# Hybrid DeltaNet / gMLP block: squares of W1 tied behind the level copies of the inverse, rows of the second MLP half loaded later

## The chip, the cores and the metric

The kernel runs on one core of a Trainium2 chip. The core has five engines that run side by side, each with its own list of instructions in a fixed order: TensorE (PE, matrix products), VectorE (DVE), ScalarE (ACT), GpSimd (POOL) and SyncE (SP, which here issues the loads and stores). The metric is the device time of one execution in microseconds; lower is better. The time before is the median of three executions.

## The reference, cut to what matters

One layer runs over 128 context tokens and 2048 latent tokens (17 tiles of 128), all in float32. What bears on the change:

```
h   = rmsnorm(x) * (1 + scale1) + shift1
qkv, gate, ab, u, vg = split(h @ w_in)
o_a = gated DeltaNet, forward and backward over chunks of 64   # triangular solve per chunk, then a scan
o_b = gelu(u) * (w_spatial @ layernorm(gelu(vg)) + b_spatial)
x   = x + gate1 * (concat(norm(o_a) * silu(gate), o_b) @ w_out)
h   = rmsnorm(x) * (1 + scale2) + shift2
x   = x + gate2 * (square(relu(h @ w_ff1)) @ w_ff2)
y   = rmsnorm(x) * norm_final
```

The outputs are the new context rows, the new latent rows and the final states of the context scan.

## The kernel before, in words

**Stages.** (1) The input stage: six blocks of up to three tiles are normalised, projected to q, k and v, convolved, and put into DRAM (`qT_d`, `kT_d`, `kt_d`, `vt_d`, and the products `kk_d`, `qk_d`). Its last steps (`decay_steps`) turn the decay inputs into cumulative sums `gcol`, transpose them on PE (L779) and store them as rows in `g_d` (L784). (2) The scan stage: a first pass over 17 units (forward direction) and a second over 17 (backward). Each unit inverts a 128 x 128 triangular matrix per head, in `prep`, by doubling levels of 2, 4, 8, 16, 32 and 64, and then takes four `scan` steps. A unit's inverse begins with the load `gb` of its decay rows from `g_d` (L1104); ACT makes `E` of it (L1166, L1167), POOL masks it, DVE multiplies it into `KK`, and a copy and a transpose later PE starts level 2 (L1218). Each level is: PE, a DVE product with a mask (L1222), PE (L1231, L1233), and two ACT copies, `Y` (L1234) and `X` (L1235); the last of these is the level copy that the change speaks of. (3) The first MLP product, in two halves of token tiles with seven products each (steps in the order 1, 5, 6, 7, 3, 2, 4 for each unit of 256 columns, class `Unit`), reading the row tiles `hop`. Step 5's sum is copied out of its bank of PSUM by ACT (L1768), and step 3 adds onto that same bank, so that step 3 waits for the copy. (4) The second MLP product.

Each product of full precision is three matmuls on split operands (`mm3`, L313 to L315).

**Fill.** While the inverses run, PE is given other products to do: in the first pass the projections to gate, u and vg from `hrow` rows (the "fill"), of which 111 matmuls stand ahead of the first inverse; in the second pass the output projection with W_out.

**Squares of W1.** The MLP's first product needs a power of two for scaling w_ff1, and with it the sum of squares over that whole matrix. So 64 pieces of 256 KB are loaded into `raw` buffers (`w1_load`, four buffers in turn, shared with W_out's pieces), and ACT squares each and sums it (`square_w1`, L247). `w1_range` takes the sum and makes the scale. Only this scale is needed, and not before the MLP.

**What sets the order.** The scan stage's steps are given times in units of a scan step (`at`), and are recorded in that order. A scheduler then orders each engine's list by its own model of time: an instruction may move ahead of one recorded earlier if its inputs are ready, unless a tie forbids it. Two helpers write ties between instructions of one engine: `behind` (behind all instructions kept under a name) and `calm` (behind the last level copy recorded on that engine). They add no wait on the chip, only an order. Before the change, loads and squares of W1 have times of 0.5 and 1.0 onward, and no tie.

**The second half's MLP rows.** The context tile's rows `h2_d[0]` are stored by `h2_steps` (L1006) and read back by `first_load` (L1808, two loads of 256 KB, each split into two 16-bit parts by ACT at L1680 and DVE at L1673). It is called 20 steps ahead of the second half (`half - 20`). The second half's `hop` tiles are loaded by `hop_next` (L1071) from step `half - 11` on.

Of the kernel before, what the change touches and what calls it, by code (L numbers as in the profile page):

```python
# [62 lines left out]
def hybrid_step(  # L63
# [121 lines left out]
    def raw_w(src, pool=None, tag="w"):  # L185
        t = (pool or wp).tile([P, 512], F32, tag=tag, name="raw")
        load(out=t, in_=src)
        return t
# [24 lines left out]
    done = {}  # L213
# [32 lines left out]
    def square_w1(n, raw):  # L246
        A.activation(raw, raw, AF.Square, accum_out=w1_sums[:, n : n + 1])  # L247
# [26 lines left out]
    def here():  # L274
        return len(tc.nc.cur_bb.bb.instructions)

    def behind(name, start, engines):

        for x in tc.nc.cur_bb.bb.instructions[start:]:
            for y in done[name]:  # L280
                if x.engine == y.engine and x.engine in engines:
                    tc.add_manual_dep(x, y.name, mybir.DependencyInfo(
                        mybir.DependencyClass.NoSync, mybir.DependencyReason.DATA), reason="order")
# [13 lines left out]
    def w512(name, dt=F32):  # L297
        return wp.tile([P, 512], dt, tag="w", name=name)
# [77 lines left out]
    with ExitStack() as ph:  # L376
# [104 lines left out]
        for t in BLOCKS[0]:  # L481
            x = pe.tile([P, D], F32, tag="x", name="x", bufs=6)
# [410 lines left out]
        for bi in range(len(BLOCKS)):  # L893
# [4 lines left out]
            at = {e: n for n, e in enumerate(order)}  # L898
            tile_of = {}
            for n, (gi, h) in enumerate(order):  # L900
                u = us[n] if bi == 0 and n < 3 else feature_tile(blk, bi, gi, h)
# [157 lines left out]
    def hop_tile(dt, n):  # L1059

        side, bufs = ("A", 2) if n else ("B", 5)
        shape = [P, 2, 4, 2, 4, P] if dt == F16 else [P, 4, 2, 4, P]
        return hops[side].tile(shape, dt, tag="hop", name="hop", bufs=bufs)

    def hop_next():
        g, o = hop_order.pop(0)
        if g == 0:
            both = hop_tile(F16, o in ORDER[:2])
            hop[0, o], hop[1, o] = both[:, 0], both[:, 1]
        for k in range(0, 4, 2):  # L1070
            load(out=hop[g, o][:, k : k + 2], in_=hop_d[g, o][:, k : k + 2])  # L1071


    with ExitStack() as ph:
# [44 lines left out]
        def calm(f, lag=0):  # L1119

            start = here()
            f()
            for x in tc.nc.cur_bb.bb.instructions[start:]:
                if x.engine in urgent and len(urgent[x.engine]) > lag:
                    tc.add_manual_dep(x, urgent[x.engine][-1 - lag].name, mybir.DependencyInfo(
                        mybir.DependencyClass.NoSync, mybir.DependencyReason.DATA), reason="order")
# [309 lines left out]
        w1_raws = {}  # L1436

        def w1_load(n):
            k, fb = divmod(n, 8)
            w1_raws[n] = raw_w(w_ff1[0, k * P : (k + 1) * P, fb * 512 : fb * 512 + 512], sp, "raw")  # L1440
# [15 lines left out]
        def load_wo(n, k):  # L1456
            if k == 0:
                ga1.append(wrow(mod_d[1:2, 2 * D + n * 512 : 2 * D + n * 512 + 512]))
                WO.append([])
            WO[n].append(load_split(w_out[0, k * P : (k + 1) * P, n * 512 : (n + 1) * 512], wscale[:, k : k + 1]))  # L1460

        def o_loads(u):
            t = u["t"]
            u["of"], u["ga"] = w512("of"), w512("ga")
            load(out=u["of"], in_=of_d[t * P : (t + 1) * P, :])
            load(out=u["ga"], in_=gate_d[t * P : (t + 1) * P, :])
# [74 lines left out]
        def at(time, fn, kind=None):  # L1541
            events.append((time, len(events), fn, kind))

        def spread(t0, t1, steps, kind):
            for j, st in enumerate(steps):
                at(t0 + (t1 - t0) * (j + 0.5) / len(steps), st, kind)

        def scan_step(i, f):
            def g():
                u = units[i]  # L1550
                if "s" not in u:
                    u["s"] = None if i in (0, NT) else units[i - 1]["sn"] if i not in (1, NT + 1) else u["s0"]
                f()
            return g

        def after(i):

            d = 0 if i == 0 else 1
            store(out=new_state[0, 0, d].rearrange("h k v -> k h v"), in_=units[i]["sn"])

        def state_load(i):

            s0 = fpart("s0").rearrange("p (h d) -> p h d", h=H)
            load(out=s0, in_=state_delta[0, 0, 0 if i == 0 else 1].rearrange("h k v -> k h v"))
            units[i + 1]["s0"] = s0

        def noted(name, f):

            start = here()
            f()  # L1570
            done[name] = tc.nc.cur_bb.bb.instructions[start:]

        def after_keys(f):

            start = here()
            f()
            behind(("kk", 1), start, (mybir.EngineType.SP,))

        p2, p3 = WINDOWS[:8], WINDOWS[8:]
        for i, u in enumerate(units):  # L1580
            w = p2 if i <= NT else p3
            at(i - 3 if i > 1 else -12.1, lambda i=i, u=u: noted(("kk", i), u["prep_loads"]))
            at(i - 3 if i > 1 else -11.1, (lambda u=u: after_keys(u["qk_load"])) if i < 2 else u["qk_load"])
            at(i - 1, u["scan_loads"])
            n = len(u["prep"])
            for j, st in enumerate(u["prep"]):
                at(i - w[0] + (j + 0.5) * (w[0] - w[1]) / n if i or j > 9 else -11.6 if j < 2
                   else 0.2 * j - 8.15, st, "prep")
            for j, f in enumerate(u["scan"]):
                shift = {2: 0.12}.get(j, 0.0) if i > NT else 0.0  # L1590
                at(i + w[2] + (w[3] - w[2]) * (j + 0.5) / 4 + shift, scan_step(i, f), "chain")
            if i in (0, NT):
                at(i - 1, lambda i=i: state_load(i))
                at(i + w[2] + (w[3] - w[2]) * 0.7, lambda i=i: after(i))
            if i >= NT:
                at(i, lambda u=u: o_loads(u))
                first, second = o_steps(u)
                spread(i + p3[4], i + p3[5], first, "fill")
                spread(i + p3[6], i + p3[7], second, "fill")
                if u["t"] > 8:  # L1600
                    st = h2_steps(u["t"], pj, fraw, w512, fpart, fhalf, lambda u=u: u["x2"])
                    spread(i + p3[8], i + p3[9] + 0.2, st[:5], "fill")
                    spread(i + p3[9] + 0.2, i + p3[9] + 2.1, [lambda f=f: calm(f) for f in st[5:]], None)
# [19 lines left out]
        flat = flat[NF:]  # L1623
        spread(p2[4], p2[5], flat, "fill")
        for n in range(64):
            at(0.5 + n * 0.24, lambda n=n: w1_load(n))
            at(1.0 + n * 0.24, lambda n=n: square_w1(n, w1_raws.pop(n)))
        at(16.5, w1_range, "fill")
        wo = [lambda n=n, k=k: load_wo(n, k) for n in range(2) for k in range(KT)]
        spread(16.75, 17.4, wo[:6], None)  # L1630
        spread(17.45, 18.2, wo[6:], None)
# [66 lines left out]
    def as4(t):  # L1698
        return t.rearrange("p (a d) -> p a d", a=4)
# [105 lines left out]
    def first_load():  # L1805
        for i in range(2):
            r = as4(w512("x0"))
            load(out=r, in_=h2_d[0][:, i * 4 : i * 4 + 4, :])  # L1808
            h, lo = split16x4(r)
            x0.extend((h[:, k, :], lo[:, k, :]) for k in range(4))  # L1810
# [264 lines left out]
    def weights_at(p):  # L2075
        if p < len(seq):
            o, n, b = seq[p]
            units[n].weights(o)

    def loads_at(p):  # L2080
        if p < len(seq) and seq[p][1] not in begun:
            begun.add(seq[p][1])
            units[seq[p][1]].loads()
# [7 lines left out]
    half = [p for p, e in enumerate(seq) if e[1] == NP][0]  # L2091
    later = []
    for j, t in enumerate(range(8, -1, -1)):
        st = h2_steps(t, bank, lambda: w512("junk"), w512)
        p = 10 + 19 * j // 2
# [7 lines left out]
    for p, (o, n, b) in enumerate(seq):  # L2103
        u = units[n]
        loads_at(p + LEAD + 8)
        weights_at(p + LEAD)
        while later and later[0][0] <= p:
            later.pop(0)[1]()
        if p == half - 20:
            first_load()  # L2110
        u.step(o)
        while firsts and firsts[0][0] <= p:
            firsts.pop(0)[2]()
        if half - 11 <= p < half + 3 and (half - p) % 2:
            hop_next()
        e = p - last
        if e >= 0 and e % 2:
            if e // 2 == 0:
                for m in range(AHEAD):
                    s_next(m, True)  # L2120
                t_ahead(0, 4)
            elif e // 2 < 5:
                for k in range(4 * (e // 2) - 4, 4 * (e // 2)):
                    t_next(0, k)
                if e // 2 <= AHEAD:
                    s_next(e // 2 - 1, False)
                    s_next(AHEAD + e // 2 - 1, True) if e // 2 < 3 else None
# [107 lines left out]
```

## Time and profile before

| what | value |
|---|---|
| time, median of 3 | 2556.02 us (2554.91 to 2556.05) |
| the profiled execution's own time | 2553.04 us |
| its span in the trace | 2551.3 us |
| PE busy | 2468.6 us, 97% |
| DVE busy | 1888.3 us, 74% |
| ACT busy | 1342.8 us, 53% |
| POOL busy | 235.7 us, 9% |
| DMA share | 67.8% of 16 engines' span |

Busy time is the time in which an engine had an instruction under way. The granted clock of TensorE is 0.988 of full speed over the span. Times below are microseconds from the span's start. An idle time in brackets is the time that the engine sat idle just before the instruction, with what ended it.

### The profile page before, as it was taken

Reading aid. Unit: us, or ns where it says so; the run is one execution under the profiler, and the core shown is the slowest. Engines: PE = TensorE matmul, PEld = TensorE weight load, DVE = VectorE, ACT = ScalarE, POOL = GpSimd, SP = SyncE. Lnnn points to the kernel's source line nnn. Section 1 sums busy time; section 2 is a strip of 40 time slices with the busy share of each in tenths; the row PEclk is TensorE's granted clock in tenths of the full one; section 3 lists DMA queues with packets and bytes.
Section 4 is the critical chain, followed back from the end, with each engine's and each line's share of the span. In section 5 each row is a group of like instructions: output and inputs, shape, how many; then the busy total and the mean of one; then the engine's idle time right before and its main releaser. Section 6 shows DMA issues by size and latency. Waiting matters only on the chain.

```text
span 2551.3 us, 44102 instructions
## 1 busy us (share of the span) xinstructions
PE 2468.6 (97%) x15188; PEld 1664.4 (65%) x15188; DVE 1888.3 (74%) x3898; ACT 1342.8 (53%) x3257; POOL 235.7 (9%) x429
## 2 busy tenths in 40 slices
PE   8999998599999999999999989999999999999998
PEld 4666666266666688778544434444467888888887
DVE  4868885387777888987688968878775557785875
ACT  3756766565555667764365645555443433243442
POOL 3112211111111111110000000000000000000000
PEclk9999999799999999999999999999999999999999
DMA  8767757844444656675567786666589979786773
GB/s 290 229 181 216 226 161 229 277 155 152 143 138 132 187 175 229 225 250 181 188 203 237 235 250 191 196 179 187 159 273 371 337 265 320 254 263 206 226 258 112
DMA packets 480487, 554.04 MB, mean 217 GB/s; under 512 B 37812, under 2 KB 284892, under 8 KB 480262
## 3 DMA queue, kind: packets, MB, share of 16 engines
q1 hardware_dynamic: 480262, 551.22, 67.8%
q8 instruction: 119, 1.95, 0.3%
q14 instruction: 106, 0.87, 0.1%
HBM read 395.00 MB, written 156.08 MB: 216 GB/s over the span
## 4 chain that ended last, share of the span: by engine, by line
PE 79%; DMA 8%; DVE 6%; ACT 4%; issue 1%; SPq 1%; POOL 1%; POOLq 0%; DVEq 0%; ACTq 0%
PE f L313 16%; PE f L314 16%; PE f L315 16%; PE pj L313 5%; PE pj L315 5%; PE pj L314 5%; PE pd L1138 5%; DMA raw<-in_w_ff_dram 2%; PE pm L313 2%; PE pm L314 2%; PE pm L315 2%; DMA QK<-qk_d 1%; PE pt L683 1%; DMA raw<-in_w_mod_dram 1%; DMA t_d<-r 1%
## 5 line engine op out<-in xcount | busy, mean ns | idle before, releaser
L313 PE MATMUL f<-hop,zH 128*128 128x512 f32 (+1 forms) x976 | 376.8, 386 | 2.1 <-ACT zH L1691 2.1
L315 PE MATMUL f<-hop,zL 128*128 128x512 f32 (+1 forms) x976 | 376.7, 386 | 0.4 <-DVE zL L1673 0.4
L314 PE MATMUL f<-hop,zH 128*128 128x512 f32 (+1 forms) x976 | 376.1, 386 | 0.0
L313 PE MATMUL f<-hop,w 128*128 128x512 f16 x896 | 340.3, 381 | 8.6 <-ACT p L1768 7.8
L314 PE MATMUL f<-hop,w 128*128 128x512 f16 x896 | 341.2, 381 | 0.0
L315 PE MATMUL f<-hop,w 128*128 128x512 f16 x896 | 339.8, 381 | 0.0
L1691 ACT CAST zH<-zraw 128x512 fp32r<-128x512 f32 x240 | 146.8, 620 | 303.9 <-DMA zraw<-s_d 91.5
L314 PEld LDWEIGHTS <-w 128*128 128x128 f16 x1536 | 151.3, 99 | 154.3 <-issue 16.1
L313 PEld LDWEIGHTS <-w 128*128 128x128 f16 x1536 | 151.1, 98 | 147.7 <-issue 3.8
L315 PEld LDWEIGHTS <-w 128*128 128x128 f16 x1536 | 151.2, 98 | 145.0 <-issue 3.5
L313 PEld LDWEIGHTS f<-hop,zH 128*128 128x128 f32 x976 | 183.4, 188 | 40.8 <-ACT zH L1691 3.8
L315 PEld LDWEIGHTS f<-hop,zL 128*128 128x128 f32 x976 | 183.4, 188 | 39.6 <-DVE zL L1673 2.9
L314 PEld LDWEIGHTS f<-hop,zH 128*128 128x128 f32 x976 | 183.4, 188 | 36.6 <-issue 0.2
L1673 DVE TENSOR_TENSOR zL<-zraw,zH 128x512 fp32r<-128x512 f32 x240 | 163.1, 687 | 58.8 <-ACT zH L1691 47.0
L313 PE MATMUL pj<-kH,w 128*128 128x386 f16 (+2 forms) x568 | 181.1, 323 | 6.3 <-ACT w L205 3.3
L314 PE MATMUL pj<-kL,w 128*128 128x386 f16 (+2 forms) x568 | 181.6, 322 | 0.0
L315 PE MATMUL pj<-kH,w 128*128 128x386 f16 (+2 forms) x568 | 180.1, 321 | 0.0
L181 POOL TENSOR_TENSOR r<-rsq,nhalf 128x1 f32<-128x1 f32 (+1 forms) x37 | 26.7, 720 | 1372.2 <-DVE rsq L180 1372.2
L1683 ACT ACTIVATE w<-s,scales 128x512 f16<-128x512 f32 x96 | 68.5, 717 | 94.5 <-DVE s L1673 94.2
L629 DVE SCALAR_TENSOR_TENSOR cv<-pj,vec,cv 128x384 f32<-128x384 f32 (+2 forms) x142 | 83.1, 589 | 32.5 <-ACT cv L627 31.1
L206 DVE SCALAR_TENSOR_TENSOR w<-raw,scales,w 128x512 f16<-128x512 f32 x112 | 81.9, 745 | 20.3 <-ACT w L205 20.3
L313 PE MATMUL pj<-w,hrow 128*128 128x512 f16 x248 | 94.5, 381 | 0.0
(459 smaller groups left out, 5455.0 us busy)
## 6 DMA issues: line engine op xcount, KB each, us to landing
raw<-in_w_ff_dram SPq DMA_DIRECT2D x256, 256.0 KB
zraw<-z_d SPq DMA_DIRECT2D x212, 256.0 KB
z_d<-c SPq DMA_DIRECT2D x96, 256.0 KB
zraw<-s_d SPq DMA_DIRECT2D x96, 256.0 KB
raw<-in_w_mod_dram SPq DMA_DIRECT2D x80, 256.0 KB
r<-in_w_ff_dram SPq DMA_DIRECT2D x80, 256.0 KB
s_d<-s SPq DMA_DIRECT2D x64, 256.0 KB
t_d<-r SPq DMA_DIRECT2D x64, 256.0 KB
```

What stands on the lines that cost most here:

```text
L181: G.tensor_tensor(out=out, in0=t[:np_, :n], in1=nhalf[:np_, :n], op=ALU.pow)
L206: V.scalar_tensor_tensor(out=t[:, 1, :], in0=raw, scalar=scale, in1=t[:, 0, :], op0=ALU.mult, op1=ALU.subtract)
L313: T.matmul(ps, lh, rh, start=first and i == 0, stop=False, skip_group_check=more)
L314: T.matmul(ps, lh, rl, start=False, stop=False, skip_group_check=more)
L315: T.matmul(ps, ll, rh, start=False, stop=last and i == n - 1, skip_group_check=more)
L629: V.scalar_tensor_tensor(out=cv, in0=ps[:, w : w + ncol - 2], scalar=convw[:, w, j : j + 1], in1=cv, op0=ALU.mult, op1=ALU.add)
L683: T.matmul(ps[:, i * P : (i + 1) * P], kTt[:, i * P : (i + 1) * P], rhs[i], start=True, stop=True)
L1138: T.matmul(p[:, h, :], lhs[:, h, :], rhs[:, h, :], start=True, stop=True)
L1673: V.tensor_tensor(out=out, in0=a, in1=b, op=op)
L1683: A.activation(h, src, AF.Copy, scale=scale)
L1691: A.copy(h, src)
```

## The change

In the scan stage, the 64 loads of W1 are given later and denser times (1.3 + 0.23 n for 0.5 + 0.24 n), and each is tied on SP behind the loads that the last recorded scan unit issues (`scan_loads`, kept under "loads"). The 64 squares follow half a step later, and each is tied behind the last level copy on ACT (`calm`). `w1_range` goes from 16.5 to 16.6. In the MLP, `first_load` goes from 20 to 16 steps ahead of the second half, and its loads and those of `hop_next` are tied on SP behind the SP instructions of the last step (`done["stored"]`).

No instruction is added or removed. Line numbers of the changed file are the same up to L1064, 6 higher from there, 12 higher from L1573 and 15 higher from L2111 on.

```diff
+    def stored_before(f):
+        start = here()
+        f()
+        behind("stored", start, (mybir.EngineType.SP,))
...
+        def after_loads(f):
+            start = here()
+            f()
+            behind("loads", start, (mybir.EngineType.SP,))
...
-            at(i - 1, u["scan_loads"])
+            at(i - 1, lambda u=u: noted("loads", u["scan_loads"]))
...
-            at(0.5 + n * 0.24, lambda n=n: w1_load(n))
-            at(1.0 + n * 0.24, lambda n=n: square_w1(n, w1_raws.pop(n)))
-        at(16.5, w1_range, "fill")
+            at(1.3 + n * 0.23, lambda n=n: after_loads(lambda: w1_load(n)))
+            at(1.8 + n * 0.23, lambda n=n: calm(lambda: square_w1(n, w1_raws.pop(n))))
+        at(16.6, w1_range, "fill")
...
-        if p == half - 20:
-            first_load()
+        if p == half - 16:
+            stored_before(first_load)
+        start = here()
         u.step(o)
+        new = [x for x in tc.nc.cur_bb.bb.instructions[start:] if x.engine == mybir.EngineType.SP]
+        done["stored"] = new or done.get("stored", [])
...
         if half - 11 <= p < half + 3 and (half - p) % 2:
-            hop_next()
+            stored_before(hop_next)
```

What this does to the order is seen best in three places. The first is the passage from the input stage to the scan stage. On SP, before, from the last W1 loads ahead of the store of the decay rows (`g_d`) to the load of these rows (`gb`):

```order
L187 DMA raw<-in_w_ff_dram 128x512 x3
L784 DMA g_d<-scr 128x128
L785 DMA g_d<-scr 8x128
L373 DMA hrow<-h_d 128x768 x2
L647 DMA vt_d<-tk 128x2x128
L1391 DMA gate_d<-th 128x512
L647 DMA vt_d<-tk 128x2x128
L373 DMA hrow<-h_d 128x768 x2
L647 DMA vt_d<-tk 128x2x128
L373 DMA hrow<-h_d 128x768 x5
L1104 DMA gb<-g_d 128x512 x2
```

And on SP now, at the same place:

```order
L687 DMA qk_d<-ev 128x2x128
L1397 DMA gate_d<-th 128x512
L784 DMA g_d<-scr 128x128
L785 DMA g_d<-scr 8x128
L647 DMA vt_d<-tk 128x2x128 x2
L1397 DMA gate_d<-th 128x512
L647 DMA vt_d<-tk 128x2x128
L1110 DMA gb<-g_d 128x512 x2
```

Forty W1 loads stood ahead of `gb` before and 24 more behind it, up to the first unit's scan; now none stands there, and the nine `hrow` loads between store and load have gone behind it. The first W1 load now comes just ahead of the store of the first unit's state, and from there about four stand to a unit. On PE the transposes of the decay rows (L779) stand behind 92 of the 111 fill matmuls before, and behind 59 now.

The second place is the ACT list inside the scan's first pass (`Y` and `X` are the copies of a level, `E` the decays of the next unit, `AH` and `P` parts of the inverse). Before, in the middle of the pass:

```order
L1234 CAST Y<-pd 128x8x32
L1235 CAST X<-pd 128x8x32
L1234 CAST Y<-pd 128x64x4
L1235 CAST X<-pd 128x64x4
L1251 ACTIVATE P_5934<-pd 64x4x64
L1192 CAST AH<-KK 128x512
```

Now, at the same instructions:

```order
L1240 CAST Y<-pd 128x8x32
L1241 CAST X<-pd 128x8x32
L247 ACTIVATE raw,w_sums<-raw 128x512
L1395 ACTIVATE gw<-pj,scales 128x512
L1240 CAST Y<-pd 128x64x4
L1241 CAST X<-pd 128x64x4
L247 ACTIVATE raw,w_sums<-raw 128x512
L1257 ACTIVATE P_5934<-pd 64x4x64
L1198 CAST AH<-KK 128x512
```

Each square stands right behind an `X` copy, and the inverse's next ACT instruction behind the square.

The third place is SP and ACT ahead of the MLP's second half (`x` is the loaded context row tile, `h_0_d` its place in DRAM, `p` the copy of step 5's or 7's sum, `c` of step 2's). ACT before:

```order
L1683 ACTIVATE w_20185<-raw,scales 128x512
L1015 CAST op<-y 128x512
L1680 CAST w_20195<-x_20193 128x512
L1680 CAST w_20200<-x_20198 128x512
L1768 ACTIVATE p_20216<-f,scales 128x512
L1683 ACTIVATE w_20218<-raw,scales 128x512
```

And ACT now, from the copy of step 5's sum on:

```order
L1780 ACTIVATE p_20206<-f,scales 128x512
L1695 ACTIVATE w_20208<-raw,scales 128x512
L1695 ACTIVATE w_20227<-s,scales 128x512
L1015 CAST op<-ev 128x512
L1787 ACTIVATE p_20248<-f,scales 128x512
L1695 ACTIVATE w_20256<-s,scales 128x512
L1695 ACTIVATE w_20279<-s,scales 128x512
L1692 CAST w_20284<-x_20282 128x512
L1692 CAST w_20289<-x_20287 128x512
L1804 ACTIVATE c_20304<-f,scales 128x512
```

The two splits of the context rows stood just ahead of the copy of step 5's sum; now they stand behind the copies of steps 5 and 7 of that unit. On SP the two loads moved in the same way: from between the two stores of the rows they read, to behind the store of `s_d` of step 3, with five other SP instructions between the last row store and them.

## Rows read from the trace of the kernel before

**Rows 1.** The page, parts 1 and 2: busy time, and busy tenths by slice.

```profile
PE 2468.6 (97%) x15188; PEld 1664.4 (65%) x15188; DVE 1888.3 (74%) x3898; ACT 1342.8 (53%) x3257; POOL 235.7 (9%) x429
...
PE   8999998599999999999999989999999999999998
```

**Rows 2.** Busy time by stretch: engines PE, PEld, DVE, ACT, POOL; clock, DMA share, GB/s.

```profile
400.00:455.60 55.60, 49.55 (x311) 30.02 (x308) 23.10 (x83) 34.71 (x117) 11.94 (x2) 0.97 0.86 269
455.60:477.20 21.60, 0.04 (x2) 0.14 (x3) 4.54 (x9) 7.15 (x20) 2.32 (x3) 0.55 0.98 316
477.20:520.00 42.80, 35.79 (x258) 18.91 (x258) 26.05 (x80) 32.06 (x91) 6.61 (x8) 0.91 0.70 229
520.00:880.00 360.00, 353.47 (x3260) 240.21 (x3258) 282.51 (x805) 208.87 (x558) 52.96 (x70) 1.00 0.48 149
...
1480.00:1530.00 50.00, 42.18 (x191) 19.07 (x190) 32.84 (x52) 19.62 (x36) 0.00 (x0) 0.93 0.77 233
```

**Rows 3.** Waits from 385 to 545: total, times, longest; PE's, then ACT's.

```profile
PE pd L1218 <- ACT Y L1234: 4.4, 4, 1.5
PE pt L642 <- ACT kn L663: 1.7, 1, 1.7
...
ACT raw L247 <- DMA raw<-in_w_ff_dram: 26.7, 23, 4.5
```

**Rows 4.** Instruction groups by form on ACT, 385 to 520: busy, mean ns, idle before.

```profile
L247 ACT ACTIVATE raw<-raw 128x512 f32<-128x512 f32 x64 | 40.1, 628 | 27.8 <-DMA raw<-in_w_ff_dram 26.7 <-DVE rsq L180 0.7
```

**Rows 5.** Timeline of SP's issues: start, duration.

```profile
453.11 3.53 SPq L187 DMA_DIRECT2D raw<-in_w_ff_dram  x3
456.74 0.38 SPq L784 DMA_DIRECT2D g_d<-scr  x1
...
464.29 0.91 SPq L1104 DMA_DIRECT2D gb<-g_d  x2
```

**Rows 6.** Timeline of PE, from the decays' transpose to the first inverse.

```profile
449.75 0.33 PE L779 MATMUL pt<-ident,gcol 128*128 128x128 f32 x1 [0.54 <-ACT tk L646]
...
455.22 0.38 PE L315 MATMUL pm<-w,hrow 128*128 128x512 f16 x1
...
477.16 0.37 PE L1218 MATMUL pd<-Y,AH 128*128 128x64 f16 x4 [21.57 <-DVE Y L1200]
```

**Rows 7.** Timeline of ACT around the first inverse.

```profile
469.38 1.28 ACT L1166 ACTIVATE E<-gb,gcol 128x128 f32<-128x128 f32 x4 [8.79 <-DMA gb<-g_d]
...
479.93 0.63 ACT L247 ACTIVATE raw<-raw 128x512 f32<-128x512 f32 x1 [4.50 <-DMA raw<-in_w_ff_dram]
...
480.56 0.37 ACT L1234 CAST Y<-pd 128x256 f16<-128x256 f32 x1
```

**Rows 8.** PE's waits in the scan's first pass, 520 to 905.

```profile
PE pd L1218 <- ACT Y L1234: 3.9, 4, 1.7
```

**Rows 9.** One line of the kernel: ACT's part of W_out's split, durations, first and last start.

```profile
L195 ACT ACTIVATE wH<-raw,wscale x16: 710/722/744, 747.6 to 880.2; 128x512 fp32r<-128x512 f32 x16
```

**Rows 10.** Timeline of SP's issues ahead of the second half.

```profile
1499.69 0.38 SPq L1006 DMA_DIRECT2D h_d<-ev  x1
...
1503.41 0.32 SPq L1808 DMA_DIRECT2D x<-h_d  x1
```

**Rows 11.** Timeline of ACT at the same place.

```profile
1502.53 0.62 ACT L1680 CAST w<-x 128x512 f16<-128x512 f32 x1 [13.08 <-DMA x<-h_d]
1506.74 0.62 ACT L1680 CAST w<-x 128x512 f16<-128x512 f32 x1 [3.59 <-DMA x<-h_d]
1507.26 0.68 ACT L1768 ACTIVATE p<-f,scales 128x512 f32<-128x512 f32 x1
```

**Rows 12.** Timeline of PE at the same place.

```profile
1499.80 0.38 PE L315 MATMUL f<-hop,w 128*128 128x512 f16 x1
1507.99 0.59 PE L313 MATMUL f<-hop,w 128*128 128x512 f16 x1 [7.82 <-ACT p L1768]
1508.37 0.63 PE L314 MATMUL f<-hop,w 128*128 128x512 f16 x1
```

## The prediction

> **What bounds the kernel now.** I read the page first: PE is busy for 97% of the span and its slices show one clear hole, in the eighth slice, and a smaller one in the 24th [rows 1]. So a change can gain only where PE idles, or where it runs at half clock after idling. Next I cut the holes out by stretches [rows 2]. Between 400.0 and 455.6 PE is busy for 49.55 of 55.6 us (6.05 idle); between 455.6 and 477.2 it does nothing (21.6 idle, granted clock 0.55); between 477.2 and 520.0 it is busy for 35.79 of 42.8 (7.0 idle, clock 0.91). That is 34.6 us of idle time at the passage from the input stage to the scan. From 520 to 880, the rest of the first scan pass, only 6.5 of 360 us are idle. In 1480 to 1530, ahead of the MLP's second half, 7.8 are idle. The MLP before and behind that shows full slices.
>
> Then the waits, which name what ends these holes. PE's 21.6 us end with the transpose `Y` of the first inverse [rows 6]. ACT, meanwhile, waited 26.7 us in 23 places for W1 loads [rows 3]. The squares sit in ACT's list between the copies that the inverse needs, so each late load holds up all that stands behind it: the square at 479.93 waited 4.50 us, and the `Y` copy behind it started at 480.56, when the square ended [rows 7].
>
> The Trainium skill, in "PSUM — Partial Sum Buffer", section "Engine vs sequencer instructions", says that ScalarE's, VectorE's and GpSimd's queues are strictly first in, first out. The copy behind the late square agrees with it. It speaks against this change too, since the squares stay on ACT and only change their neighbours: that is the second rival below.
>
> **Part one: the passage to the scan.** The 64 loads are 16.8 MB. At the 269 to 316 GB/s that the DMA moved here [rows 2] they alone take 53 to 62 us of its time between 390 and 510; they now move into a stretch that runs at 149 GB/s. The 64 squares take 40.1 us of ACT there [rows 4].
>
> First, 400 to 455.6. The longest single wait in it is 1.7 us for an ACT copy of normalised keys [rows 3], which stands among the squares, as all of ACT's work does there; about 1 us for the first `hrow` load I leave. I take 5 of the 6.05 us of idle time, plus 1 of the at most 1.7 us lost to the clock ((1 - 0.97) x 55.6). The fill then ends near 449.6 in place of 455.6.
>
> Second, the hole to 477.2. Its end is set by the decay rows: transpose on PE at 449.75, store at 456.74, load issued at 464.29, `E` at 469.38, first inverse at 477.16 [rows 5 to 7]. Before the store, SP spent 3.53 us on three W1 loads that waited for buffers [rows 5]. Now the transpose stands behind 59 of the 111 fill matmuls, not 92, so 52 and not 19 follow it. Matmuls of this form start 0.215 us apart (the one at 455.22 is the last of the 19), so the transpose goes some 7.1 us up against the fill's end: from 5.9 ahead of it to about 13, that is to 436.6. Evacuation and store take some 2 us without SP's W1 loads: 439. The load `gb` stands behind four stores, the last of which needs transposes that come 18 matmuls (3.9 us) behind: issue at about 443. From issue to `E` it took 5.1 us, and from `E` to PE 7.8 [rows 5 to 7]. That gives 455 to 456 for the first inverse; I take 455. Against 477.2 this is 22 us, which holds the first part's 6. The gap that stays is 5.4 us. Bounds: 14 us if the transpose goes up only with the fill (449.75 - 6 = 443.8) and the chain behind it keeps its 27.4 us but for the 3.5 of W1 loads and some 4.5 of nine `hrow` loads (nine issues some 0.5 us apart, as the two of `gb`), so that the inverse starts at 463; and 27 if the gap closes.
>
> In "DMA: Bandwidth & Descriptors", section "Latency and other measured facts", the Trainium skill says that a DMA's fixed cost falls with the load on HBM. Here `gb` took 5.1 us from issue to use at 316 GB/s and the context rows 3.3 (1503.41 to 1506.74) at 233 GB/s, which agrees. By it the sum would be 1 to 2 us better than I take it.
>
> Third, the first inverse, 477.2 to 520. PE's list is the same here. 7.0 us are idle, 4.4 of which end with a `Y` copy of ACT [rows 3], and up to 3.9 are lost to the clock ((1 - 0.91) x 42.8). Without squares among the copies I take 6 of these 10.9, since a gap ahead of the inverse remains and with it some time at 1.2 GHz. Bounds 2 and 9.
>
> **Part two: what the squares cost in the scan's first pass.** ACT is busy there for 208.9 of 360 us, 58% [rows 2]; 64 squares of 0.628 us [rows 4] add 40.1 us and make 69%. The cover is the time in which ACT waits for PE's next result after an `X` copy, exactly where `calm` puts a square. PE lost only 3.9 us to `Y` copies in all of the pass [rows 8]. If a quarter of the squares delays the next copy, and that by half a square, this costs PE 64 x 0.25 x 0.31 = 5 us. Bounds: below nothing, since the scheduler sets a new order here, and the pass's own 6.5 us of idle time could shrink by half (-3); above, every square on PE's path, 40 us. The value is near the low end, since a unit's inverse is spread over two and a half units of time and PE has fill between. If the cover is gone (a late W1 load holds ACT for longer than the inverse's slack), the upper end applies. SP must issue four more loads per unit, each behind the unit's own loads; at DMA share 0.48 that costs the unit's loads nothing I can price, and it is inside the bounds.
>
> The end of the pass: half of W_out's 16 pieces were split earlier, the first at 747.6 [rows 9]; now they share buffers with W1 to the end and all crowd into the last two units, 16 x 0.72 us on ACT. I count this with the 5 us above.
>
> **Part three: ahead of the second half.** The context rows were read back right behind their own store: second store at 1499.69, second load at 1503.41, split at 1506.74 [rows 10, 11]. ACT waited 13.08 and 3.59 us. Behind the splits stood the copy of step 5's sum, at 1507.26, and PE's step 3 waited 7.82 us for it; the next ten matmuls started 0.43 and not 0.215 us apart, at 1.2 GHz [rows 11, 12], 2.1 us. Now the loads come some 10 us after the stores (four steps of 12 matmuls of 0.215), and behind the splits stands no copy that PE's next two products add onto. ACT will still wait some 4 us for the loads, as they are issued only behind the store of step 3; what is late next is the copy of step 2's sum, whose bank is needed several steps later. So I take the whole 9.9 us; bounds 6 and 10.5. `hop` loads move back by several steps too, but the first is used 11 steps (28 us) after its time; I take nothing.
>
> **Sum.** 22 + 6 + 10 - 5 = 33 us off. The profiled execution took 2553.0, of which 2551.3 is the span: 2520. The median of the runs lies 3.0 us above it, so the forecast is 2556 - 33 = 2523 us. With all terms at their likely ends together this case runs from 2512 to 2535.
>
> **Rivals.**
> *The hole is the decay chain's own.* If the time from transpose to first inverse (27.4 us) hardly shrinks, the hole moves with the fill's end and only the 6 us of the first stretch, half of the third and the second half are gained: 6 + 3 + 10 - 5 = 14, 2542 us. For it: each step of that chain waits for the one before. Against it: SP spent 8 us of it on W1 and `hrow` loads that now stand elsewhere, and the transpose itself goes up.
> *The squares sit on the inverse's path.* By ACT's order each square delays the copy behind it, by its 0.63 us and by its share of load waits, 26.7 / 64 = 0.42 us [rows 3, 4], if loads are as late as at the passage: 64 x 1.05 = 67 us in place of 5, so 2556 - 38 + 67 = 2585 us, slower. It decides from 0.59 us per square on (38 / 64), about the square's whole length. For it: the squares stand between `X` and the inverse's next ACT instruction, once even ahead of the `P` of level 64. Against it: loads are issued half a unit ahead, at half the DMA load, and PE has fill in between.
> *The second half's wait comes back.* ACT's and DVE's wait behind the store of step 3 meets PE after all, with as long a stall: no gain there, 2533 us. For it: both engines again stop for a load in the middle of a step. Against it: 10 us more between store and load, and the copy of step 5's sum ahead of the splits.
>
> **How the numbers follow.** Forecast 0.72; decay chain 0.12; second half 0.10; squares on the path 0.06. The range 2508 to 2544 holds the forecast's own spread and the two rivals on the fast side, and leaves out the slower one and the tails, together under 0.2. A measurement of this kernel tells about 0.2%, 5 us, from no change. The first three cases are all faster by more than that except in their tails: faster 0.92, within it 0.03, slower 0.05.
>
> **What would show it.** In the changed profile: no hole of over 10 us before the first inverse, which starts near 455; the group of L247 spread over 520 to 870 less some 25 us, with little idle time before it; PE's idle time in the first pass not above some 12 us; no PE wait near 1470 in front of step 3. It is wrong if PE's waits for `Y` and `P` copies in the first pass sum to tens of us, if ACT's squares still wait for loads by tens of us, or if a hole near 20 us stays ahead of the first inverse.

## The result, and the profile after

The changed kernel takes 2510.99 us (median of four runs, 2507.82 to 2515.27) against 2555.47 for the kernel before (2551.42 to 2556.05): a ratio of 0.983, with a 95% interval of 0.981 to 0.985. Forecast were 2523 us, in a range of 2508 to 2544. Run again beside other kernels it took 2512.80 us against 2551.41, 38.6 us less. The two profiled executions lie 37.7 us apart in span (2551.3 and 2513.6; the second is the slowest of its four runs), and that difference can be taken apart by landmarks that both traces have.

First the page of the changed kernel, parts 1 and 2, to hold against [rows 1]:

```profile
PE 2460.9 (98%) x15188; PEld 1661.8 (66%) x15188; DVE 1887.9 (75%) x3898; ACT 1340.8 (53%) x3257; POOL 233.3 (9%) x429
...
PE   8999999899999899999999999999999999999998
```

The eighth slice, at the passage to the scan, has gone from 5 to 8, and the 24th is full. A new 8 stands in the 14th, at the end of the scan's first pass. The same instructions run: DVE's and ACT's busy times agree with before within 2 us. PE's busy time is 7.7 us lower for the same instructions, and the rest of the 37.7 us is idle time of PE that has gone.

Next the busy time by stretch, cut at the landmarks of the changed run: the end of the fill (445.7, inside the first row), the first inverse, the store of the first unit's output (`of_d`), the store of the 17th unit's, and the stretch ahead of the MLP's second half. Columns as in [rows 2].

```profile
400.00:447.00 47.00, 45.72 (x313) 30.11 (x311) 22.97 (x82) 18.73 (x61) 11.94 (x2) 1.00 0.59 177
447.00:452.80 5.80, 0.02 (x1) 0.12 (x2) 3.85 (x8) 0.62 (x1) 2.31 (x3) 0.62 0.97 364
452.80:504.20 51.40, 51.40 (x429) 30.78 (x429) 40.17 (x119) 29.05 (x73) 9.96 (x12) 0.94 0.56 182
504.20:840.50 336.30, 326.07 (x2982) 221.29 (x2978) 256.23 (x720) 222.94 (x631) 43.38 (x60) 1.00 0.60 188
1440.00:1490.00 50.00, 50.00 (x237) 23.21 (x236) 41.08 (x68) 24.87 (x46) 1.07 (x1) 1.00 0.69 207
```

The kernel before, between the same landmarks (first inverse to first store, first store to 17th):

```profile
477.20:537.80 60.60, 53.59 (x428) 31.61 (x428) 40.59 (x122) 43.33 (x121) 9.72 (x12) 0.94 0.70 226
537.80:868.10 330.30, 323.77 (x2978) 220.05 (x2974) 256.64 (x721) 188.00 (x505) 45.72 (x61) 1.00 0.46 143
```

So the change gains 24.4 us up to the first inverse (477.2 to 452.8), and 9.2 us from there to the first store, where PE's 7.0 us of idle time became none and its busy time fell by 2.2. It loses 6.0 us in the first pass (330.3 to 336.3). The second pass is 1.5 us shorter, the MLP's first product 10.2 us (from the first of its L313 matmuls to the last 646.8 and 636.6), and the rest is 1.6 us longer. The sum is 37.7.

What answers to [rows 5 to 7]: the timelines of SP, PE and ACT at the passage in the changed run, one fence each.

```profile
434.20 0.33 SPq L784 DMA_DIRECT2D g_d<-scr  x1
...
439.47 0.94 SPq L1110 DMA_DIRECT2D gb<-g_d  x2
```

```profile
433.46 0.27 PE L779 MATMUL pt<-ident,gcol 128*128 128x128 f32 x1
...
445.34 0.38 PE L315 MATMUL pm<-w,hrow 128*128 128x512 f16 x1
452.78 0.37 PE L1224 MATMUL pd<-Y,AH 128*128 128x64 f16 x4 [7.06 <-DVE Y L1206]
```

```profile
445.01 1.28 ACT L1172 ACTIVATE E<-gb,gcol 128x128 f32<-128x128 f32 x4 [1.80 <-DMA gb<-g_d]
...
450.43 0.62 ACT L1198 CAST AH<-KK 128x512 f16<-128x512 f32 x1 [3.48 <-POOL KK L1193]
```

From transpose to store it is now 0.7 us in place of 7.0, and from store to load issue 5.3 in place of 7.6. From load issue to `E` it is 5.5 us (before 5.1), and from `E` to PE 7.8 as before. The last two are the chain's own. Of the gap, 7.06 us are left. This passage repeats well: in the eleven other traces without W1's loads and squares at this place the first inverse starts between 449.5 and 453.8, behind a gap of 6.3 to 7.4 us.

The groups of squares in the scan's first pass, answering to [rows 4], with the last column for idle time before them:

```profile
L247 ACT ACTIVATE raw<-raw 128x512 f32<-128x512 f32 x64 | 41.8, 657 | 0.0
L247 ACT ACTIVATION_READ_ACCUMULATOR raw<-raw 128x1 f32 x64 | 13.9, 218 | 0.0
```

No square waits for its load any more (26.7 us before). PE's waits from 500 to 885, answering to [rows 8]:

```profile
PE pd L1237 <- DVE P L1228: 5.9, 7, 1.4
PE pd L1224 <- ACT Y L1240: 4.6, 7, 0.9
PE pd L1256 <- ACT Y L1240: 2.3, 3, 1.8
PE pd L1274 <- DVE Y L1266: 1.8, 2, 0.9
```

Many short waits, the longest 1.8 us; squares on the inverse's path at their full length would have shown as tens of microseconds (64 x 0.63 = 40).

### The profile page after: what moved, and what is told of

It is laid out like the page before. It is cut to its first block, busy times and chain, and to the rows that moved or that the text cites. A ratio compares the mean times of both kernels' runs of the same rounds, so it can differ in the third digit from the quotient of the medians.

```text
span 2513.6 us, 44064 instructions
## 1 busy us (share of the span) xinstructions
PE 2460.9 (98%) x15188; PEld 1661.8 (66%) x15188; DVE 1887.9 (75%) x3898; ACT 1340.8 (53%) x3257; POOL 233.3 (9%) x429
## 4 chain that ended last, share of the span: by engine, by line
PE 83%; DMA 7%; DVE 5%; ACT 3%; issue 1%; SPq 1%; POOL 1%; POOLq 0%; DVEq 0%; ACTq 0%
PE f L315 16%; PE f L313 16%; PE f L314 16%; PE pj L313 6%; PE pj L315 6%; PE pj L314 6%; PE pd L1144 5%; PE pm L313 2%; PE pm L314 2%; PE pm L315 2%; DMA QK<-qk_d 1%; PE pt L683 1%; DMA r<-in_w_ff_dram 1%; DMA raw<-in_w_mod_dram 1%; DMA zraw<-z_d 1%
## 5 line engine op out<-in xcount | busy, mean ns | idle before, releaser
L313 PE MATMUL f<-hop,zH 128*128 128x512 f32 (+1 forms) x976 | 377.0, 387 | 2.5 <-ACT zH L1703 2.4
L313 PE MATMUL f<-hop,w 128*128 128x512 f16 x896 | 339.4, 380 | 0.0
L313 PEld LDWEIGHTS <-w 128*128 128x128 f16 x1536 | 150.9, 98 | 146.3 <-ACT w L205 3.8
L313 PEld LDWEIGHTS f<-hop,zH 128*128 128x128 f32 x976 | 183.3, 188 | 41.6 <-ACT zH L1703 5.0
L313 PE MATMUL pj<-kH,w 128*128 128x386 f16 (+2 forms) x568 | 180.6, 322 | 6.0 <-ACT w L205 3.3
L313 PE MATMUL pj<-w,hrow 128*128 128x512 f16 x248 | 94.0, 379 | 0.0
```

The source lines that it names most:

```text
L313: T.matmul(ps, lh, rh, start=first and i == 0, stop=False, skip_group_check=more)
```

## The experiments

Each was timed in five rounds beside the kernel before (medians 2554.05, 2551.41 and 2553.55 us on the three occasions). Diffs are against the changed kernel. "The whole" is the changed kernel run again, `e5_whole_again`.

### The two parts apart

```diff
 # e1_squares_alone
-        if p == half - 16:
-            stored_before(first_load)
+        if p == half - 20:
+            first_load()
...
-            stored_before(hop_next)
+            hop_next()
 # e2_rows_alone
-            at(1.3 + n * 0.23, lambda n=n: after_loads(lambda: w1_load(n)))
-            at(1.8 + n * 0.23, lambda n=n: calm(lambda: square_w1(n, w1_raws.pop(n))))
-        at(16.6, w1_range, "fill")
+            at(0.5 + n * 0.24, lambda n=n: w1_load(n))
+            at(1.0 + n * 0.24, lambda n=n: square_w1(n, w1_raws.pop(n)))
+        at(16.5, w1_range, "fill")
```

> The W1 part of the change alone; the context rows are loaded 20 steps ahead of the second half, as before. Theory (the parts add): the passage to the scan gains its 24 + 9 us and the first pass loses 6, as between the two profiles, so some 28 us (at most 35) off before, 2521 to 2528 us, and PE's wait of about 8 us for the copy of step 5's sum (7.8 before) is there again. Rival (the rows' wait was hidden or an effect of W1's loads): the same time as the whole change, 2511 us, and no such wait.

> The MLP part alone; W1's loads and squares as before. Theory: 10 us off before, 2545 us (2543 to 2549); the hole of some 21.6 us ahead of the first inverse is there, the wait of 7.8 us ahead of step 3 is not. Rival (the later rows move their wait elsewhere): within 3 us of before.

The squares alone: 2523.91 us, 30.1 below before (ratio 0.988, 0.987 to 0.989). The rows alone: 2545.96 us, 8.1 below (0.997, 0.996 to 0.998). Together 38.2, which is what the whole gains in its repeat (38.6). The parts add; the second, 10.2 us between the first two profiles, is worth 8.1 us by these medians. Each has its own mark in the trace of PE. First e2, where the hole at the passage is back; then e1, where the wait ahead of step 3 is:

```profile
476.32 0.37 PE L1224 MATMUL pd<-Y,AH 128*128 128x64 f16 x4 [21.64 <-DVE Y L1206]
```

```profile
1478.55 0.59 PE L313 MATMUL f<-hop,w 128*128 128x512 f16 x1 [7.25 <-ACT p L1780]
```

### Which tie does it

```diff
 # e3_no_copy_tie
-            at(1.8 + n * 0.23, lambda n=n: calm(lambda: square_w1(n, w1_raws.pop(n))))
+            at(1.8 + n * 0.23, lambda n=n: square_w1(n, w1_raws.pop(n)))
 # e4_no_load_tie
-            at(1.3 + n * 0.23, lambda n=n: after_loads(lambda: w1_load(n)))
+            at(1.3 + n * 0.23, lambda n=n: w1_load(n))
```

> The whole change, but the squares are not tied behind the level copies; their loads are still tied behind a unit's loads. The scheduler then places up to four squares as a group, and one of the first ahead of the copy X of level 64's end. Theory A (the gain is the cleared passage; the place of a square in a unit is worth little): no hole over 10 us ahead of the first inverse, the first pass 3 to 8 us longer, 2514 to 2520 us. Theory B (the tie behind the copies is what keeps the squares off the inverse's path): at least 0.3 us for each of 64 squares, 2530 us or more, and PE's waits for Y and P copies of ACT in the first pass at 25 us or more.

> The whole change, but W1's loads are not tied behind a unit's loads; the squares are. ACT's, PE's and DVE's lists are those of the whole change; on SP only the first four loads (as many as there are buffers) go up to the input stage. Theory: the order of the squares holds the loads back, through their four buffers; 2511 us, within 4 us. Rival (it is the loads in SP's queue that made the hole): four loads of 256 KB are 1 MB, 3.5 us of DMA time at 300 GB/s, and come back as a longer gap ahead of the first inverse, 2515 us or more.

Without the load tie: 2515.05 us (0.985, 0.984 to 0.986), against 0.985 for the whole in its repeat. The load tie is worth nothing that can be measured, as the theory had it: squares that may not go up hold their loads back through the four buffers. Without the copy tie: 2529.22 us (0.990, 0.989 to 0.991), slower than theory A and at the edge of theory B. The passage is clear (6.35 us of idle time ahead of the first inverse), so the loads there are not what costs; the pass from first to 17th store takes 347.3 us against 335.6 for the whole's repeat (the trace of e3 is that of its fastest run, 2521.61 us). Either tie by itself clears the passage; the later times with neither tie were not tried. In e3's squares the load waits are back (durations, then what their engine waited for):

```profile
L247 ACT ACTIVATE raw<-raw x64: 612/630/677, 496.8 to 804.0; 128x512 f32<-128x512 f32 x64
...
  DMA raw<-in_w_ff_dram: 40.1, 27
```

PE's idle time in the pass is 20.4 us (347.3 less 326.85 busy) against 10.2 in the changed run's (336.30 less 326.07), in many waits of at most 2.1 us. The two largest sums are for DVE's products `P`, and for the copies `X` of level 64 (L1268), some of which stand behind squares:

```profile
PE pd L1237 <- DVE P L1228: 8.8, 9, 2.1
PE pd L1274 <- ACT X L1268: 4.0, 5, 1.3
```

The 25 us of waits for ACT's `Y` and `P` copies, theory B's second sign, did not come. ACT stood 40.1 us in front of squares, with the inverse's copies behind them. The Trainium skill's page "PSUM — Partial Sum Buffer", section "Engine vs sequencer instructions", has ScalarE's queue strictly first in, first out, and this trace agrees: with 27 late loads PE's pass is 11.7 us longer.

### What the squares and their loads still cost

```diff
 # e6_squares_doubled
-        A.activation(raw, raw, AF.Square, accum_out=w1_sums[:, n : n + 1])
+        A.copy(raw, raw); A.activation(raw, raw, AF.Square, accum_out=w1_sums[:, n : n + 1])
 # e7_no_squares
-        A.activation(raw, raw, AF.Square, accum_out=w1_sums[:, n : n + 1])
+        if n < 1: A.activation(raw, raw, AF.Square, accum_out=w1_sums[:, n : n + 1])
...
-        w1_raws = {}
+        w1_raws = {}; V.memset(w1_sums, 1.0)
 # e9_no_loads_either: e7, and
-        for n in range(64):
+        for n in range(1):
```

> The changed kernel once more, beside the others of this call and the kernel before: 2511 to 2515 us, 40 to 45 us below before.

> Ahead of each square ACT copies the piece onto itself in place, which changes no value and adds 64 instructions of some 0.62 us: 40 us more of ACT in the first pass. Theory (the squares lie mostly in the time in which ACT waits for PE): the pass got 6 us longer with 64 squares, and as ACT's load goes from 66% to 78% of it, the second helping costs more than the first, 8 to 16 us, so 2520 to 2530 us; PE's waits for Y and P in the pass go from 10 us to 20 or so. Rival (each square is on the inverse's path at a good part of its length): 0.4 us or more for each, 26 us and up, 2540 us or more.

> 63 of the 64 squares are left out (their sums are set to 1, so the scale for w_ff1 is another); all 64 loads stay. ACT has 40 us less in the first pass. Theory: the 6 us by which the first pass grew are the squares' price, so 5 to 7 us below the whole change. Rival (the loads' DMA traffic, or the order that the scheduler makes, lengthened the pass): within 3 us of the whole change.

> 63 of the 64 W1 loads and squares are left out (sums set to 1). The scan's first pass then has neither their ACT time nor their traffic nor their hold on the raw buffers. From the store of the first unit's output to that of the 14th and from there to the 17th it took 266.5 and 63.9 us before, 268.0 and 67.6 with the change, 266.6 and 67.5 without squares. Theory A (it is the four raw buffers: W_out's pieces must wait for the last W1 piece and crowd): the last three units go back to 63 to 64 us, and W_out's first split to some 40 to 70 us ahead of the 815 us of the change; 3 to 5 us below the whole change, 2508 to 2510 us. Theory B (another order of the first units' work): the last three units stay at 67 us.

The whole: 2512.80 us (0.985, 0.983 to 0.986), 38.6 us off where I expected 40 to 45. Doubled: 2516.37 (0.986, 0.984 to 0.988), below the 2520 to 2530 that I expected. Without squares: 2512.65 (0.985, 0.984 to 0.986). Without loads too: 2506.12 (0.982, 0.980 to 0.983), theory A and 2 us more. I expected 5 to 7 us from the missing squares and got none: my theory of the pass's 6 us failed. The stores of the units' outputs on SP divide the pass: from the first to the 14th, and from there to the 17th.

| kernel | 1st to 14th | 14th to 17th | first W_out split |
|---|---|---|---|
| before | 266.5 | 63.9 | 747.6 |
| the whole (repeat) | 268.0 | 67.6 | 815.3 |
| squares doubled | 268.6 | 69.4 | 817.4 |
| no squares | 266.6 | 67.5 | 789.4 |
| no loads either | 266.5 | 64.1 | 710.4 |

A square takes 0.63 us of ACT (last section), and 54 of the 64 fall into the first 13 intervals: 34 us of ACT, which cost PE 1.5 us (267.6 to 268.8 us in the six traces that have the squares there as the whole has them, against 266.5 to 266.6 in before, e7 and e9; e2, which has none there either, took 268.1, but at a granted clock of 0.99 and not 1.00). As much again in copies costs 0.6 more, which is inside that spread. The rest of the loss, 3.7 us, stands in the last three units. Without loads it is gone. Without squares it is still there, but some 2 us of e7's time in these units are lost to a stretch at the lower clock, which the whole's repeat does not have (e7 first, the repeat second), so that as much of the 3.7 may be the squares':

```profile
769.90:837.30 67.40, 62.77 (x558) 41.93 (x556) 53.76 (x145) 40.59 (x103) 9.08 (x12) 0.97 0.62 200
772.30:839.90 67.60, 62.84 (x569) 41.43 (x567) 52.82 (x145) 44.73 (x121) 8.57 (x12) 1.00 0.65 204
```

The loads hold the four `raw` buffers to the end, and W_out's 16 pieces crowd in behind them. ACT's part of W_out's split, with what ACT waited for, in the changed kernel and then in e9 (the form of [rows 9]):

```profile
L195 ACT ACTIVATE wH<-raw,wscale x16: 709/722/752, 815.8 to 854.1; 128x512 fp32r<-128x512 f32 x16
...
  DMA raw<-in_w_out_dram: 9.8, 7
```

```profile
L195 ACT ACTIVATE wH<-raw,wscale x16: 710/721/745, 710.4 to 843.4; 128x512 fp32r<-128x512 f32 x16
...
  DMA raw<-in_w_out_dram: 0.9, 1
```

In the changed run ACT waited 9.8 us for those pieces, and 8.0 in e7; in e9 it waited 0.9, and in the kernel before not at all. It is these waits that crowd ACT's list, not the number of splits: 10 of the 16 fall into the last three units before and after. All that W1 costs in the first pass is then the 5.0 us between the whole's 335.6 and e9's 330.6. SP is another suspect: in the changed run it stood 62.4 us (34 waits, 500 to 850) until a square freed a buffer, with other loads behind it in its list. Against it speaks e7, where these waits are gone and the kernel's time is the same. That the buffers, and not the traffic of two streams of loads, make W_out's pieces late is not shown by e9, which takes away both.

### Two other placings

```diff
 # e8_both_passes
-            at(1.3 + n * 0.23, lambda n=n: after_loads(lambda: w1_load(n)))
-            at(1.8 + n * 0.23, lambda n=n: calm(lambda: square_w1(n, w1_raws.pop(n))))
-        at(16.6, w1_range, "fill")
+            at(1.3 + n * 0.45, lambda n=n: after_loads(lambda: w1_load(n)))
+            at(1.8 + n * 0.45, lambda n=n: calm(lambda: square_w1(n, w1_raws.pop(n))))
+        at(30.5, w1_range, "fill")
 # e10_denser
-            at(1.3 + n * 0.23, lambda n=n: after_loads(lambda: w1_load(n)))
-            at(1.8 + n * 0.23, lambda n=n: calm(lambda: square_w1(n, w1_raws.pop(n))))
+            at(1.3 + n * 0.19, lambda n=n: after_loads(lambda: w1_load(n)))
+            at(1.8 + n * 0.19, lambda n=n: calm(lambda: square_w1(n, w1_raws.pop(n))))
```

> The loads and squares are given times 0.45 apart in place of 0.23, so that they reach through both passes of the scan, two to a unit, and the scale follows at 30.5. Theory: the first pass gets back some 3 of its 6 us, and the second pass, in which W_out's products fill PE, loses less than that: 0 to 4 us below the whole change. Rival (W_out's pieces and the squares share the four raw buffers, and W_out's pieces come later): PE waits for W_out's splits at the start of the second pass, 5 us or more above.

> Loads and squares 0.19 apart in place of 0.23: the last square at 13.8 in place of 16.3, nothing else. Five squares to a unit in place of four cost next to nothing (64 more cost 3.6 us when they were doubled). Theory A (W_out's pieces crowd at the end of the pass because W1 holds the buffers until then): their splits begin some 15 to 30 us earlier, the last three units go from 67.6 to 64 or 65, 2 to 4 us below the whole change, 2509 to 2511 us. Theory B (not the buffers): within 1 us of the whole change.

Over both passes: 2525.80 us (0.990, 0.988 to 0.991), 13.0 us slower than the whole, where I expected 0 to 4 us less. Denser: 2517.89 (0.986, 0.985 to 0.987), a difference from the whole that these intervals do not resolve. Over both passes the first comes back to 330.6 us, but the time from the 17th store to the MLP's first matmul goes from 366.2 to 384.6 us: 8.3 of these 18.4 are more busy time of PE, and 10.1 more idle time. The whole's repeat, and then e8 with the worst stretch of it:

```profile
839.90:1206.10 366.20, 356.36 (x3046) 293.81 (x3042) 310.62 (x777) 237.05 (x730) 57.14 (x70) 1.00 0.64 206
835.40:1220.00 384.60, 364.68 (x3054) 298.39 (x3052) 314.63 (x790) 258.06 (x798) 56.10 (x70) 0.98 0.67 220
855.00:880.00 25.00, 19.33 (x158) 16.25 (x159) 22.43 (x56) 16.67 (x51) 3.38 (x4) 0.73 0.79 262
```

Most of the added busy time is the clock: from 855 to 880, a stretch that begins with a wait of 2.1 us and holds two more of about 2 us, it was 0.73, which is 6.8 us of 25. The place, the start of the second pass, is the rival's, but none of these waits is for a split of W_out (they are for DVE's and ACT's `Y` and for a load `ob`), so its mechanism is not shown. In e8's first pass the last three units take 63.1 us although ACT waited 5.5 us in them for pieces of W_out, so these waits do not always cost PE time.

Denser, the last three units do go back (64.6 us, first W_out split at 770.7, and no wait of ACT for a piece of W_out in them), as the buffers would have it; but the first 13 intervals grow to 273.3 from 268.0. I expected five squares a unit to be free, as eight instructions were in the doubled run. Why not is open: no square waits for a load in that trace, and PE's idle time there grows by only 3.2 us. Neither gives a version that beats the change.

### The rows of the second half

```diff
 # e11_rows_at_20
-        if p == half - 16:
+        if p == half - 20:
 # e12_rows_untied
-            stored_before(first_load)
+            first_load()
```

> The whole change, but the second half's context rows are loaded 20 steps ahead, as before, with the tie behind the last step's stores. Theory (the time, and with it the place of ACT's splits in front of the copy of step 5's sum, makes the wait): ACT's list has the splits ahead of that copy again, PE waits some 8 us for it, 8 to 10 us above the whole change, 2521 to 2523 us. Rival (the tie behind the stores is what helps): within 3 us of the whole change.

> The whole change, but the loads of the context rows are not tied on SP behind the last step's stores; they stay 16 steps ahead. On SP one of the two loads goes ahead of the store of step 3, ACT's list is the same. Theory: within 2 us of the whole change, no wait of PE there. Rival (a load ahead of a store that waits for DVE's sum holds that store up, and with it what reads it): 3 us or more above.

Rows at 20 steps, tied: 2513.15 us (0.985, 0.983 to 0.986). My theory fell: ACT's splits stand ahead of the copy of step 5's sum again, and still PE waits only 0.27 us there:

```profile
1468.46 0.38 PE L313 MATMUL f<-hop,w 128*128 128x512 f16 x1 [0.27 <-ACT p L1780]
```

Against e1, where the stall is whole, ACT's whole list is the same, PE's is the same up to the stall, and SP's in this place is the same but for the `hop` loads, which are gone from it (e1's rows are those with - and those without a sign). The tie of the rows has moved nothing here, so that what sets e11 apart from e1 is the tie of the `hop` loads:

```
 L1820 DMA x_20193<-h_0_d 128x512
 L1006 DMA h_0_d<-ev 128x512
-L1077 DMA hop<-hop_5_d 128x2048
 L1017 DMA hop_6_d<-op 128x1024
 L1820 DMA x_20198<-h_0_d 128x512
-L1077 DMA hop<-hop_6_d 128x2048
 L1017 DMA hop_4_d<-op 128x1024
-L1077 DMA hop<-hop_4_d 128x2048
```

SP's waits ahead of the second half, in the kernel before (1470 to 1504, up to the second load of the context rows) and in e11 (1440 to 1475):

```profile
SPq L1071 <- DMA hop_d<-op: 10.2, 3, 4.3
SPq L1808 <- DMA h_d<-ev: 4.3, 2, 2.2
```

```profile
SPq L1017 <- DVE op L1016: 13.6, 4, 6.4
SPq L1820 <- DMA h_d<-ev: 2.1, 2, 1.4
```

Three `hop` loads stood right behind the stores of the rows that they read, waited 2.3 to 4.3 us for them to land, and held up all of SP behind them: the stores of the context rows too, whose data were ready. In e1 the second `ev` (the row tile that is stored) was written by ACT by 1458.9 and stored at 1470.12; in e11 by 1455.8 and stored at 1460.48: 4.7 us behind its data in place of 11.2. ACT's first split of the loaded rows follows:

```profile
1473.38 0.62 ACT L1692 CAST w<-x 128x512 f16<-128x512 f32 x1 [12.81 <-DMA x<-h_d]
```

```profile
1463.55 0.62 ACT L1692 CAST w<-x 128x512 f16<-128x512 f32 x1 [6.09 <-DMA x<-h_d]
```

The first row is e1's, the second e11's. In the Trainium skill, "Perfetto Trace Analysis", section "DMA Instruction — HWDGE (DVE, Sync)", the issuing engine's sequencer itself waits for a DMA's semaphores and takes the next instruction only after; SP's 10.2 us agree with it. Untied rows at 16 steps take 2512.01 us (0.984, 0.982 to 0.985), the same as the whole. So with the `hop` loads out of the way neither the later time (e11) nor the tie of the rows (e12) is needed. The later rows without the tie of the `hop` loads were not tried, and whether they would do by themselves stays open.

## Why the prediction was right, and where it was not

**The sum.** 33 us were forecast, 37.7 lie between the profiles, and 38.6 to 44.5 between the medians of two comparisons. The likeliest case came, with its gains at the passage and the first inverse on the high side. The first median, 2510.99, lies just below the 2512 to 2535 that this case was given; the repeat, 2512.80, lies just inside.

**The passage, 22 us forecast, 24.4 measured.** The steps hold. The decay rows' transpose went up further than taken (433.5, not 436.6) because the fill ended at 445.7 and not at 449.6. I had put the first stretch's gain at 6 us; it was 9.9. Of these, 6.05 are idle time, all there was. The other 3.8 are work done in less time (49.55 to 45.72 us), of which at most 1.7 are the clock; the remainder I can't place. The gap was 7.06 where I took 5.4, and from the issue of `gb` to PE it took 13.3 where I took 12.9. The 1 to 2 us that a lighter load on HBM would have taken off did not come: from issue to use `gb` took 5.5 us while the DMA moved 212 GB/s, and 5.1 before, while it moved 273. The rival that the hole is the decay chain's own is right for these 13.3 us of it only.

**The first inverse, 6 forecast, 9.2 measured.** The mechanism was right and the size just above its upper bound of 9: all 7.0 us of idle time went, where I had left a part of it. The other 2.2 are work done in less time; the granted clock is 0.94 in both rows, so that it explains at most about 1 us of them, and the rest I can't place. The term counted on less time at the lower clock as well; most of that did not come.

**The first pass, 5 us lost forecast, 6.0 measured.** The size was right by luck, through two errors. The step that failed is "64 x 0.25 x 0.31 = 5": the squares' own price is 1.5 us over 13 units, and their number hardly matters. The loss in the last three units, which I had counted "with the 5 us above" and given nothing of its own, is 3.7 us. e9 shows that W1's loads and squares together make it, and ACT's waits for late pieces of W_out go with it in the changed kernel, e7, e9 and e10, though not in e8; that the shared buffers make them late is argued. The rival with the squares on the path decides from 0.59 us each; the whole has 0.03 (1.5 / 54). Its mechanism is real, though: in e3, without the tie to the copies, 64 squares cost 11.7 us more than in the whole's repeat (347.3 against 335.6), 0.18 us each, with loads that come late.

**The second half, 10 forecast, 10.2 between the profiles, 8.1 by e2's median.** Right in size, wrong in cause. The failed step is "I take nothing" for the `hop` loads, beside "the context rows were read back right behind their own store". The read-back's own wait is 4.3 us of SP's time; the larger part of the delay was 10.2 us of waits of `hop` loads ahead of it in SP's list. I read ACT's wait and its releaser (`x<-h_d`), but did not ask SP what it had waited for before that load.

**What would show it.** No hole over 10 us, the first inverse near 455 (452.8), the squares between 522 and 822 with no idle time before them, no wait ahead of step 3: all hold. PE's idle time in the first pass, not above some 12 us by the forecast, was 12.2 from 500 to 850, at the limit.

## What to carry to other kernels

Work that waits for a load, put into an in-order list between steps of a serial chain, costs by its wait more than by its length: where its data are already there, 34 us of it can cost 1.5. When a load shares buffers with another stream, look at what that stream does behind it; here most of the price stood where the second stream came late. And when an engine waits for a DMA, ask the queue that issued it what it waited for in front of it: the load that is named as the releaser may only have been the next in line.

## What was not expected of the hardware

A square with its sum takes two records on ACT, 0.657 and 0.218 us on average, but the next instruction starts 0.09 us after the second one began, so that squares follow each other at 0.63 us:

```profile
707.64 0.65 ACT L247 ACTIVATE raw<-raw 128x512 f32<-128x512 f32 x1
708.18 0.21 ACT L247 ACTIVATION_READ_ACCUMULATOR raw<-raw 128x1 f32 x1
708.27 0.64 ACT L247 ACTIVATE raw<-raw 128x512 f32<-128x512 f32 x1
```

The same square was 0.628 us long at the passage and 0.657 in the pass. ACT's busy time in the first pass could go from 188 to 255 us of 330 to 338 (e9 and e6), and PE's pass grew by 7 us, 5 of them with the first half of that, which also brought W1's loads.
